# The second layer's modulation: row sums on VectorE and one matmul per condition, in place of eight matmul steps

## The chip, the core and the metric

The kernel runs on one core of a Trainium2 chip. The metric is the device time of one execution in microseconds (us); lower is better. Before the change the median of three runs is 1642.9 us (1642.58 to 1646.06).

## The reference

Two layers of a transformer trunk over 512 latent tokens (x) and 256 context tokens (ctx), width 1024, everything in fp32. Cut to what matters here:

```python
def modulation(cond, w, b):
    return jnp.split(jax.nn.silu(cond) @ w + b, 6, axis=-1)

for l in range(DEPTH):
    last = l == DEPTH - 1
    sh1, sc1, gt1, sh2, sc2, gt2 = modulation(c, w_mod[l], b_mod[l])           # for x
    csh1, csc1, cgt1, csh2, csc2, cgt2 = modulation(c_ctx, w_mod[l], b_mod[l]) # for ctx
    h  = rms_norm(x, g_norm1[l]) * (1 + sc1) + sh1
    hc = rms_norm(ctx, g_norm1[l]) * (1 + csc1) + csh1
    ...                              # projection w_in, three head groups, their norms
    x = x + gt1 * mix_out(...)       # w_o
    if not last: ctx = ctx + cgt1 * mix_out(...)
    x = x + gt2 * sq_relu_mlp(rms_norm(x, g_norm2[l]) * (1 + sc2) + sh2, w_fc1[l], w_fc2[l])
    if not last: ctx = ctx + cgt2 * sq_relu_mlp(...)
```

A modulation is thus silu(cond), a vector of 1024, times a matrix of 1024 by 6144, for two conditions (c and c_ctx) with the same matrix. In the second layer ctx gets only its first norm (csh1, csc1); its other four vectors are not used.

## The kernel before, in words

**Layout.** Activations stand transposed: 128 features on the partitions, 768 tokens (512 of x, then 256 of ctx, `SEGS`) along the row. KC = 8 blocks of 128 features make the width of 1024.

**Large products.** Weights come in chunks of 128 output features (`wraw`, 512 KB each). ScalarE (or VectorE) rounds one half at a time to `whi`, VectorE (or GpSimd, called POOL) subtracts to get `wlo`; four halves of each, so two chunks, have room. Activations are split in the same way into `hh`/`hl`, `oh`/`ol`, `gh`/`gl`. `gemm` and `steps` (L527 to L550) issue, for each of the eight blocks, three matmuls into one PSUM bank (`psmm`): hi by hi, hi by lo, lo by hi. A chunk for both kinds of token is 24 matmuls of 512 columns and 24 of 256. In the MLP, four groups `g` of eight chunks of the first product (`hh`) and eight of the second (`gh`) follow each other. The first is evacuated by `f_evac` (ScalarE `rl` and `gh`, VectorE `sqf` and `gl`), the second by VectorE, which adds into `x`.

**Modulation** (`modulation`, L406). The matrix is cut into three thirds: shift and scale of the first norm; gate of the first sub-layer and shift of the second norm; scale of the second norm and last gate. Each third has two halves of 1024 columns. For each half and each of eight row blocks, two tiles `wm` of 128x512 are loaded, and four small matmuls take the silu vectors `sil` (32 columns, two of them in use) as weights and 256 columns of `wm` each, into four groups of 32 PSUM rows of one bank `psm`; eight row blocks accumulate. These four matmuls are called a group below. Then the bank is copied out (`row`), transposed (`psmt`) and added to the bias (`modc`); for the scales `amod` is made. `mods` (L956) runs, in the first layer, thirds 1 and 2 of that layer after flags set in the projections, and right behind them all three thirds of the second layer.

**What sets the order.** The program is written out ahead by a planner. `_Model` keeps the time at which each engine would be free by a table of costs (`_Engine._cost`, L210) and delays (`WAIT`); `_Order.run` (L289) steps through generators in order of priority, and each yields a condition or a time. Higher priorities are the attention's streams (0 to 2) and the norms; `mods` has 4, `main` with the large products 5. Copies and subtractions go to the engine that the model finds free first (`quickest`, L465). At the end all instructions are issued sorted by the model's start time (`emit`, L170). So a cost in the table can move instructions everywhere after it, and each engine then runs its queue in that order. `SLACK` (3 us) and `LATE` (0.4 us) are margins added to modelled times. Loads are issued on SP's queue; `wm` has two buffers of its own, `wraw` two.

Of the kernel before, what the change touches and what calls it, by code (L numbers as in the profile page):

```python
# [8 lines left out]
F32 = mybir.dt.float32  # L9
F32R = mybir.dt.float32r  # L10
AF = mybir.ActivationFunctionType
ALU = mybir.AluOpType

P = 128
D = 1024
KC = D // P
# [12 lines left out]
V_G1, V_G2, V_GO, V_CW, V_CB, V_NQ, V_NK, V_WQ, V_WK = 0, 8, 16, 24, 30, 32, 33, 34, 35  # L29
# [3 lines left out]
M_SH1, M_SC1, M_GT1, M_SH2, M_SC2, M_GT2 = 0, 8, 16, 24, 32, 40  # L33
# [12 lines left out]
LATE = 400.0  # L46
SLACK = 3000.0


B_HI, B_LO, B_SM, B_SC, B_RM = 100.0, 400.0, 9999.0, 4000.0, 700.0  # L50
# [132 lines left out]
class _Engine:  # L183
# [26 lines left out]
    def _cost(self, op, n, outs, ins, k):  # L210
        if self._name == "PE":
            part, self._md.part = self._md.part, (ins[0].shape[0] > 64, outs[0].shape[0] > 32)
            c = 0.0 if part == self._md.part else 190.0
            if op == "transpose":
                return c + 109.0
            if ins[0].dtype == F32R:
                return c + max(n / 2.4 + 13.6, 110.0)
            return c + (4 * n / 2.4 if outs[0].shape[0] > 32 else 105.0)
        if self._name == "DMA":
            return outs[0].shape[0] * n * 4 / 360.0  # L220
        scalars = sum(1 for x in ins if x.shape[1:] == (1,) or list(x.shape[1:]) == [1]) if n > 1 else 0
        if self._name == "Activation":
            acc = 93.0 if k.get("accum_out") is not None else 0.0
            return (52.0 if ins[0].space == bass.MemoryType.PSUM else 93.0) + 0.8333 * n + 93.0 * scalars + acc
        if self._name == "Pool":
            return 149.0 + 2.104 * n + (128.0 + 0.4 * n if op == "tensor_scalar" else 0.0)
        if op == "reciprocal":
            return 69.0 + 6.25 * n
        return 69.0 + (0.52 if op == "tensor_scalar" else 1.0417) * n + 61.0 * min(scalars, 1)
# [85 lines left out]
def hybrid_trunk(ctx: ExitStack, tc: tile.TileContext, a: dict, out: bass.AP):  # L315
    nc = tc.nc
    md = _Model()
    vec, act, pool, pe, dma = (_Engine(md, e, n) for e, n in (
        (nc.vector, "DVE"), (nc.scalar, "Activation"), (nc.gpsimd, "Pool"), (nc.tensor, "PE"), (nc.sync, "DMA")))
# [5 lines left out]
    wp = _Pool(md, ctx.enter_context(tc.tile_pool(name="wp", bufs=2)), 2)  # L325
# [5 lines left out]
    psp = ctx.enter_context(tc.tile_pool(name="psp", bufs=8, space=PS))  # L331
# [3 lines left out]
    flag, res = (lambda: _Flag(md)), (lambda n: _Res(md, n))  # L335
    r_ps = res(8)
    r_pb, r_pt, r_g, r_l, r_mo, r_tb = res(3), res(2), res(NG), res(NL), res(1), res(2)
# [4 lines left out]
    def const(name, shape, src=None):  # L342
        t = cst.tile(shape, F32, name=name, tag=name)
        if src is not None:
            dma.dma_start(t, src)
        return t

    def tmp(name):
        return tp.tile([P, T], F32, name=name, tag="tmp")

    def taken(name):
        return lp.tile([P, T], F32, name=name, tag="long")

    def long(name):
        r_l.take()
        return taken(name)

    def free(t):
        r_l.give(md.last(t))

    cond, ex, sil = const("cond", [P, KC, 2], a["cond"]), tmp("ex")[:, 0:2 * KC], const("sil", [P, KC, 32])
    vecs = const("vecs", [P, DEPTH, NV], a["vecs"])
# [8 lines left out]
    ident = const("ident", [P, P], a["ident"])  # L371
    bmod = const("bmod", [P, DEPTH, 48], a["bmod"])
# [4 lines left out]
    nc.vector.memset(ones, -0.5)  # L377

    nc.vector.memset(sil, 0.0)
    ex = ex.rearrange("p (k s) -> p k s", k=KC)  # L380
    act.activation(ex, cond, AF.Exp, scale=-1.0)
    vec.tensor_scalar(out=ex, in0=ex, scalar1=1.0, scalar2=None, op0=ALU.add)
# [18 lines left out]
    modc = [const(f"modc{l}", [P, 48, 2]) for l in range(DEPTH)]  # L401
    amod = [const(f"amod{l}", [P, 2, KC, 2]) for l in range(DEPTH)]
    f_mod = {(l, i, j): flag() for l in range(DEPTH) for i in range(3) for j in range(2)}


    def modulation(l, third):  # L406
        first = l == 0 and third == 0
        yield r_mo.need()
        r_mo.take()
        q, ahead = [], [(half, k) for half in range(2) for k in range(KC)]  # L410
        for half in range(2):
            yield r_ps.need()
            r_ps.take()
            ps = psp.tile([P, 512], F32, name="psm", tag="ps")[:, 0:256]
            for k in range(KC):
                while ahead and len(q) < (KC if first else 1):
                    src = a["w_mod"][(l, third) + ahead.pop(0)]
                    if first:
                        yield r_g.need(2)
                        r_g.take(2)  # L420
                    wm = [gp.tile([P, 2, 256], F32, name="wm0", tag="g") if first
                          else wp.tile([P, 2, 256], F32, name="wm", tag="wm") for _ in range(2)]
                    for i in range(2):
                        dma.dma_start(wm[i], src[:, 2 * i:2 * i + 2, :])
                    if first and len(ahead) == KC:
                        f_first.set(0.0)
                    if first and not ahead:
                        f_late.set()
                    q.append(wm)
                wm = q.pop(0)  # L430
                yield md.at(*wm) + (0.0 if first else SLACK)
                for j in range(4):
                    pe.matmul(ps[32 * j:32 * j + 32, :], lhsT=sil[:, k, :], rhs=wm[j // 2][:, j % 2, :], start=k == 0,
                              stop=k == KC - 1)
                if first:
                    r_g.give(k=2)
            yield r_l.need()
            row = long("row")
            vec.tensor_copy(row[:, 0:256], ps)
            r_ps.give(md.last(ps))  # L440
            yield md.at(row[:, 0:256])
            yield r_ps.need()
            r_ps.take()
            pt = psp.tile([P, 512], F32, name="psmt", tag="ps")
            for m in range(2):
                pe.transpose(pt[:, P * m:P * m + P], row[:, P * m:P * m + P], ident)
            free(row)
            pv = pt[:, 0:256].rearrange("p (m i j s) -> p i j m s", m=2, i=2, j=2)
            for i in range(2):
                c = third * 16 + 8 * i + 4 * half  # L450
                vec.tensor_tensor(out=modc[l][:, c:c + 4, :].rearrange("p (j m) s -> p j m s", j=2), in0=pv[:, i, :, :, 0:2],
                                  in1=bmod[:, l, c:c + 4].rearrange("p (j m s) -> p j m s", j=2, s=1).to_broadcast([P, 2, 2, 2]),
                                  op=ALU.add)
            which, col, g = {0: (0, M_SC1, V_G1), 2: (1, M_SC2, V_G2)}.get(third, (None, 0, 0))
            if which is not None:
                col, g, c = col + 4 * half, g + 4 * half, slice(4 * half, 4 * half + 4)
                for s in range(2):
                    vec.scalar_tensor_tensor(out=amod[l][:, which, c, s], in0=modc[l][:, col:col + 4, s], scalar=1.0,
                                             in1=vecs[:, l, g:g + 4], op0=ALU.add, op1=ALU.mult)
            f_mod[l, third, half].set()  # L460
            r_ps.give(md.last(pt))
        r_mo.give()


# [59 lines left out]
    def next_chunk():  # L524
        return unused.pop(0)
# [68 lines left out]

    def room(x):

        yield md.slot("DVE", max(md.t, md.ready(x, "DVE", False)), 69.0 + 61.0 + 1.0417 * x.shape[1], [x]) - B_RM

    def norm_tiles():
        return [[hp.tile([P, T], F32R, name=nm, tag="h") for _ in range(KC)] for nm in ("hh", "hl")]  # L600
# [352 lines left out]
                add_square(acc, xs0[k], s0, s1, k == 0)  # L953
            od.spawn(norm(0, 0, xs0, acc, hh, hl, s, SEGS[s], rd[s], True), s)

    def mods(l, f1, f2):  # L956
        yield f1
        if l == 0:
            yield from modulation(l, 1)
        yield f2  # L960
        if l == 0:
            yield from modulation(l, 2)
        if l + 1 < DEPTH:
            for third in range(3):
                yield from modulation(l + 1, third)

    def main():
        for l in range(DEPTH):
# [15 lines left out]
        for l in range(DEPTH):  # L984
            last = l == DEPTH - 1
            w = S if last else T
# [95 lines left out]
                     "b": lambda i: (segs, conv_evac(2, i), 0)}  # L1082
            seq = [kinds[c](i) for c, i in SEQ]

            f_m = flag(), flag()
            od.spawn(mods(l, *f_m), 4)
            att = attention_streams(l, last, units, o_done)

# [80 lines left out]
            xs, acc = [None] * KC, long("acc")  # L1169
# [61 lines left out]
            for g in range(4):  # L1231
# [26 lines left out]
                    c0 = 2  # L1258
                for c in range(c0, KC):
                    wt = next_chunk()  # L1260
                    for sg in segs:
                        yield from gemm(wt, hh, hl, sg, f_evac(c), sg is segs[-1])

                lastg = g == 3
                if lastg and not last:
# [3 lines left out]
                    acc = long("acc")  # L1269
# [126 lines left out]
```

## Time and profile before

| | |
|---|---|
| median of three runs | 1642.9 us |
| profiled execution | 1646.77 us |
| its span, first to last instruction | 1645.0 us |
| TensorE (PE) busy | 1586.5 us, 96% |
| VectorE (DVE) busy | 1002.1 us, 61% |
| ScalarE (ACT) busy | 705.9 us, 43% |
| POOL busy | 135.3 us, 8% |
| mean granted TensorE clock | 0.989 |

The profiled execution is one run among others, so its own time is given beside its span; differences are made against it. Busy times of matmuls overlap, since a matmul starts before the one ahead has ended; what a matmul costs in a full queue is read from the starts of its neighbours. The first layer's projections and attention run from 31 to 333 us, its w_o stage to 414, its MLP to about 994 us; then the second layer follows, with its own MLP from 1281 us.

### The profile page before, as it was taken

The page shows a single profiled execution, that of the slowest core. Times are in us where ns is not written, and L with a number is a line of the kernel's source. Part 1 is how long each engine was busy: PE and PEld are TensorE (multiplying, and loading weights), DVE is VectorE, ACT ScalarE, POOL GpSimd, SP SyncE. Part 2 cuts the span into 40 slices and gives each one's busy share as a digit, 9 for nine tenths or more (in the row PEclk, how much of TensorE's full clock was granted, in tenths as well). Part 3 has the DMA queues.
Part 4 walks back from the last instruction along what each step waited for, and adds up shares of the span by engine and source line. Part 5 has one row for each costly group of instructions (what it writes and reads, how often), then busy time and mean ns, then how long its engine had stood idle before and what let it go on. Part 6 is the DMA issues. An engine that isn't in the chain of part 4 may idle for free.

```text
span 1645.0 us, 24426 instructions
## 1 busy us (share of the span) xinstructions
PE 1586.5 (96%) x9210; PEld 1311.4 (80%) x9210; DVE 1002.1 (61%) x2030; ACT 705.9 (43%) x1415; POOL 135.3 (8%) x183
## 2 busy tenths in 40 slices
PE   5999999999999999999999998999999899999999
PEld 2787888778788888888888887777879788888887
DVE  4799998966743243334334458899987754545452
ACT  4677776744431122122113346667665422323231
POOL 1002121120000000000000001122212000000000
PEclk9999999999999999999999999999999999999999
DMA  9332322345433333333311243312125232323233
GB/s 330 120 118 91 119 65 79 118 153 196 147 120 115 117 106 126 110 121 104 128 65 65 84 147 115 83 52 78 42 68 174 96 103 90 103 90 103 90 103 102
DMA packets 75718, 182.25 MB, mean 111 GB/s; under 512 B 9424, under 2 KB 15824, under 8 KB 75600
## 3 DMA queue, kind: packets, MB, share of 16 engines
q1 hardware_dynamic: 75600, 180.69, 33.5%
q8 instruction: 72, 1.18, 0.3%
q14 instruction: 46, 0.38, 0.1%
HBM read 170.43 MB, written 5.24 MB: 107 GB/s over the span
## 4 chain that ended last, share of the span: by engine, by line
PE 67%; DVE 14%; ACT 5%; issue 3%; DMA 2%; POOL 0%; SPq 0%; DVEq 0%; ACTq 0%; POOLq 0%
PE psmm L207 61%; DVE pb L207 3%; PE psm L207 2%; DVE ptl L207 2%; ACT pb L207 1%; PE pso L207 1%; DVE o L207 1%; PE pst L207 1%; DVE wlo L207 1%; PE sc L207 1%; DVE hl L207 1%; DVE t L207 1%; DVE sm L207 1%; PE psr L207 1%; DVE tn L207 1%
## 5 line engine op out<-in xcount | busy, mean ns | idle before, releaser
L207 PE MATMUL psmm<-hh,whi 128*128 128x512 f32 (+1 forms) x1264 | 461.8, 365 | 10.9 <-ACT hh L207 4.3
L207 PE MATMUL psmm<-hl,whi 128*128 128x512 f32 (+1 forms) x1264 | 446.3, 353 | 1.5 <-DVE hl L207 0.8
L207 PE MATMUL psmm<-hh,wlo 128*128 128x512 f32 (+1 forms) x1264 | 445.4, 352 | 0.9 <-DVE wlo L207 0.7
L207 ACT ACTIVATE whi<-wraw 128x512 fp32r<-128x512 f32 x323 | 202.9, 630 | 426.2 <-PE psmm L207 403.3
L207 DVE TENSOR_TENSOR wlo<-wraw,whi 128x512 fp32r<-128x512 f32 x357 | 246.9, 694 | 127.5 <-ACT whi L207 124.0
L207 PEld LDWEIGHTS psmm<-hh,whi 128*128 128x128 f32 x1264 | 241.4, 191 | 59.9 <-issue 21.6
L207 PE MATMUL psmm<-gh,whi 128*128 128x512 f32 (+1 forms) x768 | 274.8, 358 | 0.0
L207 PE MATMUL psmm<-gh,wlo 128*128 128x512 f32 (+1 forms) x768 | 272.1, 354 | 0.7 <-DVE wlo L207 0.7
L207 PE MATMUL psmm<-gl,whi 128*128 128x512 f32 (+1 forms) x768 | 272.0, 354 | 0.0
L207 PEld LDWEIGHTS psmm<-hh,wlo 128*128 128x128 f32 x1264 | 240.9, 191 | 35.5 <-DVE wlo L207 3.3
L207 PEld LDWEIGHTS psmm<-hl,whi 128*128 128x128 f32 x1264 | 241.6, 191 | 30.7 <-DVE hl L207 3.5
L207 DVE SCALAR_TENSOR_TENSOR x<-psmm,modc,x 128x512 f32<-128x512 f32 (+1 forms) x96 | 63.5, 661 | 191.6 <-PE psmm L207 191.5
L207 PEld LDWEIGHTS psmm<-gh,whi 128*128 128x128 f32 x768 | 145.2, 189 | 28.2 <-issue 8.9
L207 PEld LDWEIGHTS psmm<-gh,wlo 128*128 128x128 f32 x768 | 145.1, 189 | 21.5 <-DVE wlo L207 1.1
L207 ACT ACTIVATE rl<-psmm 128x512 f32<-128x512 f32 (+1 forms) x98 | 50.9, 519 | 257.2 <-PE psmm L207 257.1
L207 PEld LDWEIGHTS psmm<-gl,whi 128*128 128x128 f32 x768 | 145.3, 189 | 19.5 <-issue 0.2
L207 DVE TENSOR_TENSOR sqf<-rl 128x512 f32<-128x512 f32 (+1 forms) x98 | 58.3, 594 | 151.7 <-ACT rl L207 148.3
L207 ACT ACTIVATE pb<-pb,mn 128x513 f32<-128x513 f32 (+3 forms) x96 | 72.1, 752 | 62.8 <-DVE mn L207 57.0
L207 POOL TENSOR_TENSOR acc<-acc,sq 128x256 f32<-128x256 f32 x34 | 30.5, 897 | 676.1 <-ACT sq L207 600.7
L207 PE MATMUL psmm<-oh,whi 128*128 128x256 f32 (+1 forms) x256 | 82.4, 322 | 0.0
L207 PE MATMUL psmm<-oh,wlo 128*128 128x256 f32 (+1 forms) x256 | 79.9, 312 | 2.2 <-DVE wlo L207 2.2
L207 PE MATMUL psmm<-ol,whi 128*128 128x256 f32 (+1 forms) x256 | 79.8, 312 | 0.0
(142 smaller groups left out, 2097.8 us busy)
## 6 DMA issues: line engine op xcount, KB each, us to landing
wraw<-in_w_fc SPq DMA_DIRECT2D x134, 512.0 KB, 3.5
wm<-in_w_mod SPq DMA_DIRECT2D x192, 256.0 KB, 3.9
wraw<-in_w_in SPq DMA_DIRECT2D x33, 512.0 KB, 3.5
wraw<-in_w_o SPq DMA_DIRECT2D x27, 512.0 KB, 3.5
tb<-in_namask SPq DMA_DIRECT2D x24, 256.0 KB, 2.8
sw<-qg SPq DMA_DIRECT2D x40, 64.0 KB, 2.0
kl<-kl SPq DMA_DIRECT2D x12, 192.0 KB, 2.5
x<-in_xT SPq DMA_DIRECT2D x8, 256.0 KB, 4.5
```

Source lines behind the costliest of these rows:

```text
L207: self._md.log.append((s, len(self._md.log), lambda: f(*a, **k)))
```

## The change

In the second layer a new generator `modulation_sums` takes the place of `modulation`. For each tile `wm` VectorE multiplies by the silu value of its row and adds to an accumulator `macc` of 128x512: one TENSOR_SCALAR for the first row block and seven SCALAR_TENSOR_TENSOR for the others, per accumulator, with two accumulators per half and condition. The sum over the 128 partitions is then done by four matmuls per half and condition, with a column of ones as weights (set in an unused place of `sil`). The first third is made for both conditions, the other two for c alone. What follows (`vectors`) is the old tail of `modulation`, moved into a function. The second layer's modulation starts on a new flag, set at the fifth chunk of the first layer's MLP. The planner's cost of a small matmul is 175 ns instead of 105, and the width in `room` is written as 512 where it was the argument's.

```diff
-            return c + (4 * n / 2.4 if outs[0].shape[0] > 32 else 105.0)
+            return c + (4 * n / 2.4 if outs[0].shape[0] > 32 else 175.0)
...
+    nc.vector.memset(sil[:, 6, 16:17], 1.0)
...
+    def modulation_sums(l, third, conds):
+        yield r_mo.need()
+        r_mo.take()
+        tiles = [(half, i, k) for half in range(2) for i in range(2) for k in range(KC)]
+        loaded, onec = [], sil.rearrange("p k s -> p (k s)")
+        def load():
+            if tiles:
+                half, i, k = tiles.pop(0)
+                wm = wp.tile([P, 2, 256], F32, name="wm", tag="wm")
+                dma.dma_start(wm, a["w_mod"][l, third, half, k][:, 2 * i:2 * i + 2, :])
+                loaded.append(wm)
+        load()
+        for half in range(2):
+            accs = {}
+            for i in range(2):
+                for s in conds:
+                    yield r_l.need()
+                    accs[i, s] = long("macc")[:, 0:512]
+                for k in range(KC):
+                    load()
+                    wm = loaded.pop(0)
+                    yield md.ready(wm, "DVE", False) + SLACK
+                    for s in conds:
+                        yield from room(wm)
+                        w, acc = wm.rearrange("p a c -> p (a c)"), accs[i, s]
+                        if k == 0:
+                            vec.tensor_scalar(out=acc, in0=w, scalar1=sil[:, k, s:s + 1], scalar2=None, op0=ALU.mult)
+                        else:
+                            vec.scalar_tensor_tensor(out=acc, in0=w, scalar=sil[:, k, s:s + 1], in1=acc, op0=ALU.mult,
+                                                     op1=ALU.add)
+            yield md.at(*accs.values()) + LATE
+            yield r_ps.need()
+            r_ps.take()
+            ps = psp.tile([P, 512], F32, name="psm", tag="ps")[:, 0:256]
+            for s in conds:
+                for j in range(4):
+                    pe.matmul(ps[32 * j:32 * j + 32, :], lhsT=onec[:, 208 - s:240 - s],
+                              rhs=accs[j // 2, s][:, 256 * (j % 2):256 * (j % 2) + 256], start=s == conds[0], stop=s == conds[-1])
...
+            yield from vectors(l, third, half, ps)
+        r_mo.give()
...
-        yield md.slot("DVE", max(md.t, md.ready(x, "DVE", False)), 69.0 + 61.0 + 1.0417 * x.shape[1], [x]) - B_RM
+        yield md.slot("DVE", max(md.t, md.ready(x, "DVE", False)), 69.0 + 61.0 + 1.0417 * 512, [x]) - B_RM
...
-    def mods(l, f1, f2):
+    def mods(l, f1, f2, f3):
...
         if l + 1 < DEPTH:
+            yield f3
             for third in range(3):
-                yield from modulation(l + 1, third)
+                yield from modulation_sums(l + 1, third, (0, 1) if third == 0 else (0,))
...
+                    if g == 0 and c == 4:
+                        f_m[2].set()
```

How it moves instructions shows at three places. On TensorE, in the first layer's MLP before, a group of four small matmuls stands between the matmuls of a chunk (here of the first product):

```order
L207 MATMUL psmm<-hh,whi 128x256
L207 MATMUL psmm<-hl,whi 128x256
L207 MATMUL psmm<-hh,wlo 128x256
L207 MATMUL psm<-wm,sil 32x256 x4
L207 MATMUL psmm<-hh,whi 128x256
L207 MATMUL psmm<-hl,whi 128x256
```

There are 48 such groups between the w_o stage and the MLP's end. On TensorE in the same stage now, the chunks hold no group, and at the end of each half one join stands, of eight matmuls in the first third and of four in the others:

```order
L207 MATMUL psmm<-gl,whi 128x512
L207 MATMUL psmm<-gh,wlo 128x512
L207 MATMUL psm<-macc,sil 32x256 x8
L207 MATMUL psmm<-gh,whi 128x512
L207 MATMUL psmm<-gl,whi 128x512
L207 MATMUL psmm<-gh,wlo 128x512
L207 MATMUL psmt<-ident,row 128x128 x2
```

There are six joins, the last some 440 matmul instructions ahead of the second layer's first norm. On VectorE, in the second product of the first MLP group, before:

```order
L207 SCALAR_TENSOR_TENSOR x_1121<-psmm,modc_112,x_1121 128x512
L207 TENSOR_TENSOR wlo<-wraw,whi 128x512
L207 SCALAR_TENSOR_TENSOR x_1121<-psmm,modc_112,x_1121 128x256
L207 TENSOR_TENSOR wlo<-wraw,whi 128x512
L207 SCALAR_TENSOR_TENSOR x_1132<-psmm,modc_112,x_1132 128x512
```

And there now, up to the end of the first half:

```order
L207 SCALAR_TENSOR_TENSOR x_1131<-psmm,modc_113,x_1131 128x512
L207 TENSOR_TENSOR wlo<-wraw,whi 128x512
L207 SCALAR_TENSOR_TENSOR x_1131<-psmm,modc_113,x_1131 128x256
L207 TENSOR_TENSOR wlo<-wraw,whi 128x512
L207 SCALAR_TENSOR_TENSOR macc<-wm,sil,macc 128x512 x4
L207 COPY row<-psm 128x256
L207 SCALAR_TENSOR_TENSOR x_1142<-psmm,modc_113,x_1142 128x512
```

Each chunk has gained four sums here; in the second and third third it is two. The copy of the join's result stands right behind the last sums. On TensorE at the end of the first layer's attention (`pso` is its last product, `psmm<-hh` the projections), before:

```order
L207 MATMUL pso<-pth,vst 128x256
L207 MATMUL pso<-ptl,vst 128x256
L207 MATMUL psm<-wm,sil 32x256 x4
L207 MATMUL psmm<-hh,whi 128x256
L207 MATMUL psmm<-hl,whi 128x256
```

And now:

```order
L207 MATMUL pso<-pth,vst 128x256
L207 MATMUL pso<-ptl,vst 128x256
L207 MATMUL psr<-acc,ones 128x256
L207 MATMUL psmm<-hh,whi 128x512
L207 MATMUL psmm<-hl,whi 128x512
```

Behind the last `pso` and ahead of the w_o stage stood 24 projection matmuls of 512 columns and 33 of 256; now it is 54 and 72. In the second layer TensorE's order differs only in its first rows, and VectorE's in eight spots.

## Rows read from the trace of the kernel before

**Rows 1.** Page, busy us, share of span, instructions:
```profile
PE 1586.5 (96%) x9210; PEld 1311.4 (80%) x9210; DVE 1002.1 (61%) x2030; ACT 705.9 (43%) x1415; POOL 135.3 (8%) x183
```
**Rows 2.** Stretches: length, busy PE, PEld, DVE, ACT, POOL; clock, DMA share, GB/s:
```profile
41.00:333.00 292.00, 284.66 (x1899) 235.76 (x1900) 262.28 (x638) 203.77 (x469) 43.53 (x66) 1.00 0.32 102
414.00:994.00 580.00, 576.79 (x3467) 479.65 (x3459) 244.48 (x435) 153.20 (x275) 7.43 (x8) 1.00 0.33 111
```
**Rows 3.** Tiles `psm` and `wm`, 400 to 830 us: durations ns, first and last start:
```profile
L207 PE MATMUL psm<-wm,sil x384: 379/391/404, 405.1 to 824.6; 128*32 128x256 f32 x192
...
DMA to landing us min/median/max: 2.5/3.9/5.3
```
**Rows 4.** TensorE's timeline around one group: start us, us, instruction:
```profile
539.99 0.40 PE L207 MATMUL psmm<-gl,whi 128*128 128x512 f32 x1
540.22 0.39 PE L207 MATMUL psmm<-gh,wlo 128*128 128x512 f32 x1
540.54 0.64 PE L207 MATMUL psm<-wm,sil 128*32 128x256 f32 x8
541.11 0.50 PE L207 MATMUL psmm<-gh,whi 128*128 128x512 f32 x1
541.45 0.39 PE L207 MATMUL psmm<-gl,whi 128*128 128x512 f32 x1
```
**Rows 5.** Stretches of eight chunks, instructions of `psmm`, then of `psm`:
```profile
567.13:640.43 73.30, 69.30 (x386) 58.36 (x385) 0.48 (x1) 7.48 (x15) 1.00 0.35 115
857.94:924.66 66.72, 66.72 (x386) 59.06 (x385) 0.48 (x1) 7.48 (x15) 1.00 0.19 64
...
567.13:640.43 73.30, 5.11 (x64) 1.26 (x64) 0.42 (x1) 1.00 0.35 115
```
**Rows 6.** TensorE's timeline at the start, four groups in one piece:
```profile
14.27 3.10 PE L207 MATMUL psm<-wm,sil 128*32 128x256 f32 x32
```
**Rows 7.** Groups by form on VectorE, 414 to 994 us; the last of the whole span:
```profile
L207 DVE TENSOR_TENSOR wlo<-wraw,whi 128x512 fp32r<-128x512 f32 x141 | 97.0, 690 | 42.3 <-ACT whi L207 40.8
L207 DVE SCALAR_TENSOR_TENSOR x<-psmm,modc,x 128x512 f32<-128x512 f32 x32 | 24.0, 751 | 129.0 <-PE psmm L207 129.0
L207 DVE TENSOR_TENSOR sqf<-rl 128x512 f32<-128x512 f32 x32 | 22.2, 693 | 135.1 <-ACT rl L207 135.1
...
L207 DVE SCALAR_TENSOR_TENSOR x<-psmm,modc,x 128x256 f32<-128x256 f32 x31 | 15.0, 483 | 6.2 <-PE psmm L207 6.1
L207 DVE CAST whi<-wraw 128x512 fp32r<-128x512 f32 x31 | 13.8, 444 | 1.7 <-PE psmm L207 0.8
L207 DVE TENSOR_TENSOR sqf<-rl 128x256 f32<-128x256 f32 x32 | 13.6, 426 | 3.3
...
L207 DVE SCALAR_TENSOR_TENSOR tn<-x,amod,acc 128x512 f32<-128x512 f32 x8 | 5.9, 746 | 0.0
...
L207 DVE TENSOR_SCALAR pb<-pb,sm 128x512 f32<-128x512 f32 x48 | 24.2, 503 | 1.6
```
**Rows 8.** TensorE's timeline at the start of the MLP, idle time in brackets:
```profile
413.82 0.64 PE L207 MATMUL psm<-wm,sil 128*32 128x256 f32 x8
...
417.78 0.48 PE L207 MATMUL psmm<-hh,whi 128*128 128x512 f32 x1 [2.12 <-DVE whi L207]
```
**Rows 9.** TensorE's waits, 414 to 994 us: us, times, longest:
```profile
PE psmm L207 <- DVE wlo L207: 0.9, 2, 0.7
```
**Rows 10.** TensorE's timeline, last attention product and first w_o matmul:
```profile
320.05 0.28 PE L207 MATMUL pso<-ptl,vst 128*128 128x256 f32 x1
...
333.14 0.40 PE L207 MATMUL psmm<-oh,whi 128*128 128x512 f32 x1
```
**Rows 11.** Stretch 420 to 940 us as in rows 2; VectorE's timeline at 405.80:
```profile
420.00:940.00 520.00, 519.88 (x3149) 431.55 (x3148) 206.18 (x375) 126.78 (x231) 0.00 (x0) 1.00 0.32 106
...
405.80 1.23 DVE L207 SCALAR_TENSOR_TENSOR tn<-x,amod,acc 128x512 f32<-128x512 f32 x1
```

More of the change, by code (lines that the diff above doesn't have):

```diff
@@ L403, in hybrid_trunk, with vectors @@
     f_mod = {(l, i, j): flag() for l in range(DEPTH) for i in range(3) for j in range(2)}
+    def vectors(l, third, half, ps):
+        yield r_l.need()
+        row = long("row")
+        vec.tensor_copy(row[:, 0:256], ps)
+        r_ps.give(md.last(ps))
+        yield md.at(row[:, 0:256])
+        yield r_ps.need()
+        r_ps.take()
+        pt = psp.tile([P, 512], F32, name="psmt", tag="ps")
+        for m in range(2):
+            pe.transpose(pt[:, P * m:P * m + P], row[:, P * m:P * m + P], ident)
+        free(row)
+        pv = pt[:, 0:256].rearrange("p (m i j s) -> p i j m s", m=2, i=2, j=2)
+        for i in range(2):
+            c = third * 16 + 8 * i + 4 * half
+            vec.tensor_tensor(out=modc[l][:, c:c + 4, :].rearrange("p (j m) s -> p j m s", j=2), in0=pv[:, i, :, :, 0:2],
+                              in1=bmod[:, l, c:c + 4].rearrange("p (j m s) -> p j m s", j=2, s=1).to_broadcast([P, 2, 2, 2]),
+                              op=ALU.add)
+        which, col, g = {0: (0, M_SC1, V_G1), 2: (1, M_SC2, V_G2)}.get(third, (None, 0, 0))
+        if which is not None:
+            col, g, c = col + 4 * half, g + 4 * half, slice(4 * half, 4 * half + 4)
+            for s in range(2):
+                vec.scalar_tensor_tensor(out=amod[l][:, which, c, s], in0=modc[l][:, col:col + 4, s], scalar=1.0,
+                                         in1=vecs[:, l, g:g + 4], op0=ALU.add, op1=ALU.mult)
+        f_mod[l, third, half].set()
+        r_ps.give(md.last(pt))
@@ new lines, in modulation_sums @@
+    def modulation_sums(l, third, conds):
[12 more added lines that the diff above has]
+            accs = {}
+            for i in range(2):
+                for s in conds:
+                    yield r_l.need()
+                    accs[i, s] = long("macc")[:, 0:512]
[12 more added lines that the diff above has]
+            yield md.at(*accs.values()) + LATE
+            yield r_ps.need()
+            r_ps.take()
+            ps = psp.tile([P, 512], F32, name="psm", tag="ps")[:, 0:256]
[3 more added lines that the diff above has]
+                              rhs=accs[j // 2, s][:, 256 * (j % 2):256 * (j % 2) + 256], start=s == conds[0], stop=s == conds[-1])
+            for t in accs.values():
+                free(t)
+            yield from vectors(l, third, half, ps)
+        r_mo.give()
@@ L436, in modulation @@
                     r_g.give(k=2)
[L437 to L461, printed above, removed]
+            yield from vectors(l, third, half, ps)
         r_mo.give()
@@ L1083, in main @@
             seq = [kinds[c](i) for c, i in SEQ]
-            f_m = flag(), flag()
+            f_m = flag(), flag(), flag()
             od.spawn(mods(l, *f_m), 4)
```

## The prediction

> **What bounds the kernel now.** I read the page's first part, the busy time by engine, to see which engine fills the span: TensorE is busy 96% of it [rows 1]. An average over stages can mislead, so the second view is the table of stretches. The first layer's MLP runs from 414 to 994 us; TensorE is busy 576.8 of those 580 us at granted clock 1.00, VectorE only 244.5 [rows 2]. The attention before it (41 to 333) looks different: VectorE is busy 262.3 of 292 us, TensorE 284.7. So in the MLP time is a sum over TensorE's queue, and in the attention two engines are close to full.
>
> Third, the instructions of tile `psm` from 400 to 830 us: 384 matmul records [rows 3]. The timeline shows eight records to one group (four instructions, one for each group of 32 PSUM rows) [rows 4], so 384/8 = 48 groups: 3 thirds by 2 halves by 8 row blocks, all of the second layer's modulation. Every one stands in the first layer's w_o stage or MLP.
>
> **What one group costs.** Its busy time is the wrong number, since records overlap. I take it from neighbours' starts. Two matmuls of 512 columns follow each other by 540.22 - 539.99 = 0.23 us. Across a group, the last one before starts at 540.22, the second after at 541.45: 1.23 us, where two steps would be 0.46. The group costs 0.77 us [rows 4]. A check from another view: eight chunks with 64 `psm` records (8 groups) take 73.30 us, eight with none 66.72, with the same 386 matmuls of `psmm` in both [rows 5]. That is 6.58/8 = 0.82 us a group, one pair of transposes included.
>
> **Removed.** 48 x 0.77 = 37.0 us of TensorE's queue.
>
> **Added on TensorE.** 32 matmuls: six joins, two of eight instructions (two conditions in the first third) and four of four. A join of four costs 0.77 as before. For eight, the second four must be bounded: 0.57 us, the start of the group to the next matmul [rows 4], or 3.10/4 = 0.78 where 32 records ran in one piece at the start of the program [rows 6]. I take the middle, 0.67: 4 x 0.77 + 2 x (0.77 + 0.67) = 6.0 us, ends 5.8 and 6.2. The Trainium skill, page "TensorEngine Tiling (Array Packing)", section "Key Properties", says that changing the tiling mode drains the engine; by it the second four, in the same mode, pay no change, and the joins come to 5.8, against 6.2 if every four paid alike. [Rows 4] side with the rule, [rows 6] do not, and it moves the sum by 0.2 us.
>
> Net on TensorE: 37.0 - 6.0 = 31.0 us.
>
> **What of that is not on the path.** One stall of 2.12 us stands at 417.78, where TensorE waits for VectorE's `whi` in the second norm [rows 8]. VectorE is held there by the norm's own chain, so two groups ahead of it (405.1 and 413.8) [rows 3, 8] only filled a wait. In the changed order that place has none: I count 2 x 0.77 = 1.5 us as not won. Ends: 0 (VectorE gets there earlier too) and 2.1.
>
> **Added on VectorE.** 16 sums of eight terms: 16 TENSOR_SCALAR and 112 SCALAR_TENSOR_TENSOR of 128x512. The first kind took 503 ns in this shape, the second 746 ns (`tn<-x,amod,acc`, all operands in SBUF like the new one) [rows 7]: 8.0 + 83.6 = 92 us. VectorE has 580 - 244.5 = 335 us free in the stage, so the question is only whether it is free at the right moments. The order puts four sums into each of 16 chunks and two into each of 32. A chunk of the first product costs VectorE two `wlo` (1.38), one `whi` (0.44), `sqf` of both widths (0.69 + 0.43) and `gl`, the same shapes, put at the same 1.12: 4.1 us. With four sums it is 7.1, and TensorE needs 66.72/8 = 8.34 us for the chunk. A chunk of the second product has two `wlo` and two `x` (0.75 + 0.48): 2.6, with four sums 5.6. So this work lies beside TensorE, with 1.2 us to spare in the tightest chunk. A delay of one burst of sums (3 us) also meets cover: weights are split two chunks ahead (about 8 us), and `gl` of the last chunk is wanted only after seven of eight row blocks of the next product, some 21 x 0.23 = 4.8 us. If that cover went, TensorE would wait by the excess.
>
> **The new wait.** At each join TensorE waits for VectorE's last sum, and behind it stand all later matmuls. The planner leaves a margin of 0.4 us (`LATE`). Ends: nothing, as VectorE's other hand-overs in the stage (0.9 us of waiting for `wlo` in 580 us) [rows 9], and one late sum at each, 6 x 0.75 = 4.5. I take 1.0, near the row. `COPY row<-psm` then holds VectorE's queue until the join is through, about 1.5 us; that is inside the spare time above.
>
> The same six halves keep their transposes and small additions, so these cancel. DMA bytes are the same. The tile loads now wait for VectorE instead of TensorE on SP's queue; each landed in 3.9 us, 5.3 at most [rows 3], issued one tile ahead, which fits into a chunk with two tiles.
>
> **The clock.** 414 to 994 runs at 1.00 [rows 2], and the eight chunks without these groups run at 1.00 too [rows 5]. No term.
>
> **What the re-planning does.** The planner's cost for small matmuls goes from 105 to 175 ns, so the first layer's attention is laid out anew, although its work is the same. In the order the last `pso` now has 54 projection matmuls of 512 columns and 72 of 256 behind it, against 24 and 33 before: 54 x 0.23 + 72 x 0.12 = 21.1 us of TensorE work instead of 9.5 (the step of 256 is what a chunk leaves: (8.34 - 24 x 0.23)/24 = 0.12). Before, 13.1 us lie between the two events [rows 10]. If the attention now ends as much sooner, nothing changes; TensorE idles 7.3 us in all of that stage [rows 2], which is the most there is to win. If VectorE sets the attention's length, TensorE runs dry for up to 21.1 - 9.5 = 11.6 us. I take 0, because TensorE's own work fills 97% of the stage, with ends -7.3 and +11.6. In the second layer TensorE's order is unchanged nearly throughout and VectorE's differs in eight spots: 0.
>
> **Sum.** 31.0 - 1.5 - 1.0 = 28.5 us. The profiled execution took 1646.8 us (span 1645.0, 1.8 outside): 1646.8 - 28.5 = 1618.3. It lies 3.9 above the median of the runs, 1642.9; on that scale 1614.4 us. That is what I forecast.
>
> **Rivals.**
> 1. The attention pays. VectorE decides its length and the moved projections find TensorE idle: 1614.4 + 11.6 = 1626. For it: VectorE is busy 90% of the stage. Against: TensorE is busy 97% there, so most of the moved work has no idle time to leave. Chance 14%.
> 2. The new layout is better: the 7.3 us of idle time halve or go, 1614.4 - 7.3 = 1607. Less work of the projections and of the group norms falls together near 330 us. Chance 9%.
> 3. VectorE's queue becomes the bound in the MLP, the slower side. A sum at its head waits for its tile, and `wlo`, `sqf` and `x` behind wait with it. Each chunk has two tiles. With a wait w per tile, the tightest chunks need 7.1 + 2w against 8.34, eight of them; the others of four sums 5.6 + 2w, eight; the 16 first-product chunks of two sums 5.6 + 2w. At w = 1.65 us this loses 16 + 4 + 9 = 29 us and eats the gain; at w = 2 it is about 22 + 10 + 20 = 52, so 1614.4 + 52 = 1666. Against: 3.9 us of landing within a chunk of 8.34. The sums can also stretch: one SCALAR_TENSOR_TENSOR took 1.23 us at 405.80 near work of POOL. POOL has 0.00 us from 420 to 940 [rows 11], so nothing stretches them there. The Trainium skill, "SBUF — State Buffer", says that a VectorE operation with two SBUF inputs and a GpSimd operation lock each other out of a shared port for a whole instruction, a rule against moving work to VectorE; by it too, an idle POOL costs nothing. Chance 4%.
> 4. The change does not bring what it says, because the MLP is paced by its weights and not by TensorE: about 1643. Against it stand the 66.72 and 73.30 us [rows 5]. Chance 2%.
>
> The forecast has 71%, with its own range 1609 to 1621: the ends above for TensorE, the stall and the joins make it 1612 to 1619, and 2.5 us either way are for a layout that is nearly neutral. The range that should hold the time 8 times in 10 adds most of rivals 1 and 2: 1606 to 1625. A measurement of this kernel tells about 0.2%, 3.3 us, from no change. Faster: forecast and rivals 1 and 2, 94%. Same: rival 4 and the middle of rival 3, 3%. Slower: the rest of rival 3, 3%.
>
> **What the profile of the changed kernel would show.** Eight chunks of the MLP with sums beside them take about 67.5 us, not 73.3. `macc` operations take about 0.75 us and VectorE is some 335 us busy in the MLP. TensorE waits for `macc` under 0.75 us at each of six joins. The second layer's stages keep their lengths. From 41 to 333 us, the order's new layout ends the projections within 7 us of where they ended. I would be wrong if TensorE shows waits for `wlo`, `gl` or `x` in the MLP, if a group turns out to have hidden something else behind it, or if the attention moved by more than its 7 us of idle time.

## The result, and the profile after

The changed kernel takes 1630.62 us (median of four runs, 1629.09 to 1631.59); the kernel before, timed beside it, took 1644.48 (1642.58 to 1646.62). The ratio is 0.9915, with an interval of 0.9897 to 0.9932. The gain is 13.9 us, where 28.5 were forecast, and the time lies above the range.

The page's first part, busy us by engine, against [rows 1]:

```profile
PE 1561.1 (96%) x8890; PEld 1313.7 (81%) x8890; DVE 1089.0 (67%) x2159; ACT 704.3 (43%) x1414; POOL 137.3 (8%) x184
```

TensorE has 320 matmul records less (a small matmul leaves two), VectorE 129 instructions more and 86.9 us more work. The stretches, columns as in [rows 2]: the attention, the MLP, eight MLP chunks with sums and a join of eight, eight with sums and a join of four, and 60 us in the attention's middle:

```profile
41.00:344.00 303.00, 287.99 (x1893) 238.15 (x1893) 268.85 (x643) 205.20 (x474) 47.71 (x70) 0.99 0.30 97
421.00:976.00 555.00, 549.43 (x3155) 479.63 (x3154) 326.08 (x561) 153.00 (x275) 9.79 (x9) 0.99 0.36 118
...
499.74:567.91 68.17, 68.17 (x404) 59.58 (x403) 42.48 (x71) 10.30 (x17) 1.29 (x1) 1.00 0.38 124
...
704.28:772.02 67.74, 67.74 (x397) 59.33 (x395) 40.80 (x72) 21.14 (x39) 0.00 (x0) 1.00 0.37 121
...
100.00:160.00 60.00, 53.48 (x365) 43.63 (x365) 54.34 (x145) 43.54 (x104) 10.21 (x20) 0.96 0.33 106
```

The third and fourth lines are the change at work: 68.17 and 67.74 us, where eight chunks took 73.30 with the groups and 66.72 with none [rows 5]. The last line is the trouble. The same 60 us before:

```profile
100.00:160.00 60.00, 59.31 (x398) 48.40 (x397) 54.50 (x141) 45.04 (x107) 10.20 (x18) 1.00 0.32 100
```

VectorE is as busy as it was (54.3 and 54.5), but TensorE runs 5.8 us less, at a granted clock of 0.96. The attention's end, against [rows 10]: the last attention product and the first w_o matmul on TensorE's timeline.

```profile
318.57 0.28 PE L207 MATMUL pso<-ptl,vst 128*128 128x256 f32 x1
...
344.36 0.40 PE L207 MATMUL psmm<-oh,whi 128*128 128x512 f32 x1
```

The attention itself ends 1.5 us sooner (318.57 against 320.05), but the moved projections then take 25.8 us where 13.1 stood. By the starts of the stages' first matmuls in the two profiled executions (spans 1645.0 and 1629.8), the difference of 15.2 us is: start -0.7, projections and attention +12.0, w_o -4.6, MLP -24.0, second layer +2.2. The w_o stage and the MLP together give 28.6, as much as the whole kernel was to gain, and the attention took 12.0 of it back.

Where it waits: TensorE's longest waits from 41 to 344 us (what waited, for what, us in all, times, longest; `sc` are scores, `pst` and `pstc` transposes of the probabilities).

```profile
PE pstc L207 <- DVE t L207: 2.5, 1, 2.5
PE sc L207 <- DVE o L207: 1.4, 1, 1.4
PE pst L207 <- DVE pb L207: 1.3, 3, 0.5
PE sc L207 <- DVE ptl L207: 1.2, 1, 1.2
PE psmm L207 <- ACT hh L207: 1.2, 1, 1.2
```

Before, in its stretch 41 to 333, the list was headed by:

```profile
PE psr L207 <- ACT sqq L207: 1.5, 2, 1.1
PE psmm L207 <- DVE ptl L207: 1.1, 1, 1.1
PE psr L207 <- DVE ptl L207: 0.8, 1, 0.8
PE pst L207 <- DVE t L207: 0.5, 2, 0.3
```

Summed over the stage from 41 us on, TensorE's waits of over 0.15 us make 14.5 us, against 6.6; 11.0 and 4.6 of them end with VectorE. The longest wait can be read step by step. First TensorE's timeline, then VectorE's up to the same moment:

```profile
151.11 0.65 PE L207 MATMUL psr<-sqq,heads 128*128 128x256 f32 x2
...
153.27 0.28 PE L207 MATMUL scx<-kl,qst 128*128 128x256 f32 x1
156.03 0.47 PE L207 MATMUL pstc<-ident,pbc 128*128 128x128 f32 x1 [2.48 <-DVE t L207]
```

```profile
151.54 0.69 DVE L207 TENSOR_TENSOR wlo<-wraw,whi 128x512 fp32r<-128x512 f32 x1
152.51 0.16 DVE L207 TENSOR_TENSOR sm<-sm 128x1 f32<-128x1 f32 x1 [0.28 <-ACT sm L207]
...
153.63 0.35 DVE L207 TENSOR_SCALAR pbc<-pbc,sm 128x256 f32<-128x256 f32 x1
153.90 0.68 DVE L207 TENSOR_TENSOR sw<-sw,sinT 128x512 f32<-128x512 f32 x1
154.69 0.69 DVE L207 TENSOR_TENSOR qg<-t,sw 128x512 f32<-128x512 f32 x1
155.29 0.68 DVE L207 SCALAR_TENSOR_TENSOR t<-psr,t 128x512 f32<-128x512 f32 x1
156.01 0.69 DVE L207 SCALAR_TENSOR_TENSOR sqq<-t,sqq 128x512 f32<-128x512 f32 x1
```

The transposes `pstc` wait until VectorE has read a `psr` out of PSUM (`t<-psr,t`). VectorE comes to that at 155.29, behind a weight split, a softmax's sums and two operations of a rotation, with hardly a gap between them. VectorE had as much to do as before; it did it in an order that made TensorE wait. Before, the same 20 `pstc` between 118 and 198 us waited for nothing. At the end of this wait the granted clock fell to its lower level, 1.2 GHz, for 6.8 us:

```profile
155.40:162.20 6.80, 5.88 (x15) 4.53 (x16) 5.86 (x12) 3.42 (x7) 0.18 (x1) 0.50 0.19 70
```

Matmuls of 512 columns follow each other by 0.43 us there (158.02 and 158.45) and by 0.23 from 162.51 on. At half speed the 6.8 us lose 3.4 us at most, since the wait itself reaches into them.

In the MLP the new parts are the accumulators (tile `macc`, durations min/median/max ns, first and last start), and TensorE's waits from 421 to 976:

```profile
L207 DVE SCALAR_TENSOR_TENSOR macc<-wm,sil,macc x112: 739/747/1532, 476.9 to 875.2; 128x512 f32<-128x512 f32 x112
...
L207 PE MATMUL psm<-macc,sil x64: 378/379/404, 538.0 to 876.9; 128*32 128x256 f32 x64
L207 DVE TENSOR_SCALAR macc<-wm,sil x16: 479/481/483, 474.7 to 841.8; 128x512 f32<-128x512 f32 x16
```

```profile
PE psmm L207 <- ACT hh L207: 3.1, 2, 2.7
PE psmm L207 <- ACT whi L207: 1.3, 1, 1.3
PE psmm L207 <- DVE wlo L207: 0.6, 2, 0.4
PE psmt L207 <- DVE row L207: 0.3, 1, 0.3
```

No wait for `macc` is among them. The 2.7 for `hh` belongs to the layout: it falls into the second norm, and VectorE's timeline ahead of it shows two pairs of the MLP's own operations put before the norm's last `tn`:

```profile
436.84 0.69 DVE L207 TENSOR_TENSOR sqf<-rl 128x512 f32<-128x512 f32 x1
437.64 0.69 DVE L207 TENSOR_TENSOR gl<-sqf,gh 128x512 fp32r<-128x512 f32 x1
438.25 0.69 DVE L207 TENSOR_TENSOR sqf<-rl 128x512 f32<-128x512 f32 x1
439.04 0.69 DVE L207 TENSOR_TENSOR gl<-sqf,gh 128x512 fp32r<-128x512 f32 x1
439.65 0.48 DVE L207 SCALAR_TENSOR_TENSOR tn<-x,amod,acc 128x256 f32<-128x256 f32 x1
```

### The profile page after: what moved, and what is told of

Same layout as the page of the kernel before. It is cut to its first block, busy times and chain, and to the rows that moved or that the text cites. A ratio compares the mean times of both kernels' runs of the same rounds, so it can differ in the third digit from the quotient of the medians.

```text
span 1629.8 us, 23969 instructions
## 1 busy us (share of the span) xinstructions
PE 1561.1 (96%) x8890; PEld 1313.7 (81%) x8890; DVE 1089.0 (67%) x2159; ACT 704.3 (43%) x1414; POOL 137.3 (8%) x184
## 4 chain that ended last, share of the span: by engine, by line
PE 70%; DVE 15%; ACT 7%; DMA 5%; issue 3%; SPq 0%; POOL 0%; DVEq 0%; ACTq 0%; POOLq 0%
PE psmm L207 64%; DVE pb L207 3%; PE pso L207 2%; DVE ptl L207 2%; ACT pb L207 1%; DVE wlo L207 1%; DMA wm<-in_w_mod 1%; PE pst L207 1%; ACT hh L207 1%; PE sc L207 1%; DVE hl L207 1%; PE psr L207 1%; DVE tn L207 1%; DVE o L207 1%; DMA wraw<-in_w_o 1%
## 5 line engine op out<-in xcount | busy, mean ns | idle before, releaser
L207 PEld LDWEIGHTS psmm<-gh,wlo 128*128 128x128 f32 x768 | 145.2, 189 | 20.9 <-DVE wlo L207 0.8
L207 DVE SCALAR_TENSOR_TENSOR macc<-wm,sil,macc 128x512 f32<-128x512 f32 x112 | 81.3, 754 | 1.0 <-DMA wm<-in_w_mod 0.2
```

The lines of the kernel that those rows point to most:

```text
L207: self._md.log.append((s, len(self._md.log), lambda: f(*a, **k)))
```

## The experiments

The theory: the sums are worth what was forecast, and the loss comes from the planner's new cost of 175 alone, because it lays out the attention anew. The first rival to it: the sums cost TensorE something in the MLP that the forecast missed. A second question is what in the new layout costs the time: the projection work left behind the last `pso` (rival 1 of the prediction), or VectorE's order ahead of it. Each kernel was timed beside the kernel before, which took 1644.0 us next to the first four kernels below and 1645.51 next to the last four.

**The sums in the old layout** (the change, with the old cost and the old slot in `room` for everything that existed before; TensorE's order is that of before up to the MLP).

```diff
-            return c + (4 * n / 2.4 if outs[0].shape[0] > 32 else 175.0)
+            return c + (4 * n / 2.4 if outs[0].shape[0] > 32 else 105.0)
...
-        yield md.slot("DVE", max(md.t, md.ready(x, "DVE", False)), 69.0 + 61.0 + 1.0417 * 512, [x]) - B_RM
+        yield md.slot("DVE", max(md.t, md.ready(x, "DVE", False)), 69.0 + 61.0 + 1.0417 * (512 if len(x.shape) > 2 else x.shape[1]), [x]) - B_RM
```

> The change with the planner's two numbers left as before (105 ns for a small matmul, the width in `room` as it was for the callers that were there): only the row sums on VectorE and their joins are new, and the first layer's attention is laid out as before. If the re-planned attention took the missing part of the gain: first w_o matmul at 333 us as before, MLP about 24 us shorter than before, 26 to 29 us faster in all. If the sums themselves bring only half of what was forecast (fillers of waits, contention on VectorE): 13 to 16 us faster, like the changed kernel.

Measured: 1615.11 us (1613.37 to 1616.78), ratio 0.9826 [0.9811, 0.984]: 28.9 us faster than before and 15.5 faster than the change as made. It is the best complete version here. Its stretches, columns as in [rows 2]:

```profile
100.00:160.00 60.00, 59.40 (x398) 48.44 (x398) 54.53 (x141) 45.03 (x107) 10.18 (x17) 1.00 0.32 101
...
691.25:759.00 67.75, 67.75 (x396) 59.31 (x395) 40.80 (x72) 21.15 (x39) 0.00 (x0) 1.00 0.36 121
```

The middle of the attention is that of before, and up to the w_o stage every engine's order in the trace is that of before (VectorE has one memset more); the eight chunks are those of the changed kernel. So the loss isn't in the sums.

**The cost alone**, in the kernel before:

```diff
-            return c + (4 * n / 2.4 if outs[0].shape[0] > 32 else 105.0)
+            return c + (4 * n / 2.4 if outs[0].shape[0] > 32 else 175.0)
```

> The kernel before with only the planner's cost of a small matmul at 175 ns: no sums. If the re-planned attention is the loss: first w_o matmul near 344 us, MLP as before (about 579 us), 8 to 11 us slower in all. If the re-planning is neutral and the sums are at fault: no difference.

Measured: 1658.95 us (1656.69 to 1660.49), ratio 1.0091 [1.0076, 1.0106]: 15.0 us slower, with no instruction added or removed. The middle of its attention, and the two events of [rows 10]:

```profile
100.00:160.00 60.00, 53.00 (x369) 43.31 (x368) 54.53 (x147) 43.70 (x104) 10.23 (x20) 0.98 0.33 107
```

```profile
318.04 0.28 PE L207 MATMUL pso<-ptl,vst 128*128 128x256 f32 x1
...
343.82 0.40 PE L207 MATMUL psmm<-oh,whi 128*128 128x512 f32 x1
```

The two halves of the change add up: 28.9 - 15.0 = 13.9, which is what the whole gained; each has an interval of some 2.5 us either way. The width in `room` was not tried by itself. TensorE's order up to the w_o stage is here that of the changed kernel but for two `psr`, and VectorE's differs in some operations of the norms, so little is left for the width to do.

The loss is larger than the 8 to 11 us expected. The profiled execution was the fastest of the four and shows 9.9 us of it: start of the projections +1.2, attention +9.5, w_o -4.6, MLP +5.8, second layer -1.9. The MLP was expected to stay as it was; its 5.8 us lie mostly in its first eight chunks (below).

**The groups not issued.** The kernel before, planned as it was, but of each half's eight groups of the second layer's modulation the first seven (42 in all) are planned and not issued; the modulation's vectors of the second layer are therefore not the reference's.

```diff
-                    pe.matmul(ps[32 * j:32 * j + 32, :], lhsT=sil[:, k, :], rhs=wm[j // 2][:, j % 2, :], start=k == 0,
-                              stop=k == KC - 1)
+                    o, w = ps[32 * j:32 * j + 32, :], {"lhsT": sil[:, k, :], "rhs": wm[j // 2][:, j % 2, :]}
+                    if l > 0 and k < KC - 1:
+                        md.op("PE", *pe._parse("matmul", (o,), w))
+                    else:
+                        pe.matmul(o, start=k == 0 or l > 0, stop=k == KC - 1, **w)
```

> The kernel before, its order kept, but of the second layer's modulation only the last of eight row blocks is issued on TensorE, in each of the six halves (the planner still counts all; the modulation is then wrong by the seven missing blocks). 42 groups of 0.77 us leave TensorE's queue, 32.3 us, and VectorE gains no work. If a group costs 0.77 us wherever it stands: 31 to 32 us faster. If the groups ahead of and within the second norm's waits only fill those waits: about 6 of them bring nothing, 26 to 28 us faster. The difference of this kernel and the first one, beyond the joins, is what the sums on VectorE cost.

Measured: 1614.69 us (1614.14 to 1616.88), ratio 0.9826 [0.9811, 0.984]: 29.3 us for 42 groups, 0.70 each overall, between the two cases expected. By the price of 0.77 they are 32.3, so some 3 us of them filled waits, where 1.5 were assumed; the interval is some 2.4 us either way. The stretch of its MLP that answers to the one above, columns as in [rows 2]:

```profile
690.46:758.21 67.75, 67.75 (x396) 59.31 (x395) 30.94 (x59) 21.16 (x39) 0.00 (x0) 1.00 0.38 125
```

It holds one group instead of a join of four, and no sums: the same 67.75 us with 9.9 us less on VectorE. Over the whole kernel it is 0.4 us faster than the sums in the old layout, inside the intervals. The sums cost TensorE nothing that these runs can tell.

**Another cost, 120**, in the sums' old layout, to see whether 175 is special (the edit is against that kernel, as are the next two):

```diff
-            return c + (4 * n / 2.4 if outs[0].shape[0] > 32 else 105.0)
+            return c + (4 * n / 2.4 if outs[0].shape[0] > 32 else 120.0)
```

> As the first kernel, with the cost at 120 ns. In this order 69 matmuls of 512 and 72 of 256 columns of the projections stand behind the last `pso`, 24.3 us of TensorE work, where the order before has 9.4 and the changed one 20.9. If what is left behind the attention decides, because VectorE sets the attention's length: first w_o matmul at 333 + 15 = 348 us, 11 to 15 us slower than the first kernel. If the loss at 175 was one unlucky place and not the left-over work: within 4 us of the first kernel.

Measured: 1634.94 us (1633.1 to 1636.48), ratio 0.995 [0.9933, 0.9966]: 19.8 us slower than with 105. The work left behind the last `pso` is 24.3 us against 9.4, which would explain 15. Its 60 us from 160 on show what else there is: TensorE busy 51.95, and the clock at 0.89.

```profile
160.00:220.00 60.00, 51.95 (x340) 42.36 (x341) 51.99 (x131) 34.94 (x87) 7.99 (x12) 0.89 0.33 106
```

**Cost 100**, and **another pace** (`B_SC` of 4000 halved: the margin by which scores are issued ahead of a free VectorE or ScalarE; cost 105), both in the same kernel:

```diff
-            return c + (4 * n / 2.4 if outs[0].shape[0] > 32 else 105.0)
+            return c + (4 * n / 2.4 if outs[0].shape[0] > 32 else 100.0)
```

> The row sums with the cost at 100 ns: 36 matmuls of 512 and 48 of 256 columns stand behind the last `pso`, 13.9 us, against 9.4 at 105. If the work left behind decides: first w_o matmul at 333.4 + 4.5 = 338 us, 3 to 5 us slower than the sums in the old layout. If the layout's loss is chance: 333 or any other value up to 344.

```diff
-B_HI, B_LO, B_SM, B_SC, B_RM = 100.0, 400.0, 9999.0, 4000.0, 700.0
+B_HI, B_LO, B_SM, B_SC, B_RM = 100.0, 400.0, 9999.0, 2000.0, 700.0
```

> The row sums at cost 105 with the attention paced differently: the margin `B_SC`, by which scores are issued ahead of a free VectorE, at 2 us instead of 4. 24 matmuls of 512 and 24 of 256 stand behind the last `pso`, 8.3 us instead of 9.4. If the work left behind decides: the first w_o matmul within 2 us of 332, the time the same as that of the sums in the old layout or up to 2 us less. If the margin was what kept VectorE fed: last `pso` later and the kernel 3 us or more slower.

Measured: 1621.47 us (1619.63 to 1623.32), ratio 0.9852 [0.9831, 0.9873], and 1639.88 us (1638.93 to 1640.9), ratio 0.9964 [0.995, 0.9977]. Cost 100 leaves 13.9 us over, 4.5 more than 105, and its attention takes 9.0 more. The halved pace leaves the least of all, 8.3, and its attention takes 14.1 more. So the left-over work does not set the stage's length.

**Less work on VectorE**, in the new layout (cost 175) and in the old one. The first 18 chunks are planned as before, but their `wlo` is not made, and the third matmul reads `whi` in its place; the projections of the first layer thus lack the weights' low part. POOL's share of these subtractions goes too.

```diff
-                minus(lo, src, hi.bitcast(F32))
+                c.no_lo = c in chunks[:18]
+                if c.no_lo:
...
+                    md.op(eng._name, *eng._parse("tensor_tensor", (), k))
+                else:
+                    minus(lo, src, hi.bitcast(F32))
...
+            if w.no_lo:
...
+                               nc.tensor.matmul(ps, lhsT=h, rhs=x, start=False, stop=e)))
+            else:
+                pe.matmul(ps, lhsT=lo[:, kc], rhs=ah[k][:, s0:s1], start=False, stop=k == end)
```

> The changed kernel (cost 175, `room` as before) with the same taken away: 23 subtractions of 0.69 us, 15.9 us, less on VectorE. If VectorE sets the attention's length and TensorE runs dry beside it: last `pso` from 318.6 to about 304, idle time of TensorE in the stage from 15 to under 5 us, first w_o matmul from 344 to 331 to 334, some 10 us or more gained, twice or three times what the old layout gains. If the new order's own waits are the loss: under 4 us gained.

> The row sums in the old layout, order kept, but the first layer's 18 projection chunks make no `wlo` (the third matmul of each block reads `whi` instead, so these products are off by their low part). 24 subtractions of 0.69 us leave VectorE, 16.6 us, and 12 leave POOL; TensorE has as many matmuls as before. If VectorE sets the attention's length: last `pso` near 304 to 310 us instead of 320, but the first w_o matmul only at 328 to 330 instead of 333.4, since TensorE has just 5.4 us of idle time to give there. If the attention's length comes from the order and its chains of waits: both move by less than 3 us.

Measured: 1621.33 us (1620.85 to 1621.82), ratio 0.9851 [0.9833, 0.9869], and 1609.9 us (1608.66 to 1611.15), ratio 0.9782 [0.9762, 0.9801]. The attention stage gains 10.5 us in the new layout (314.1 to 303.6) and 5.0 in the old (302.3 to 297.3). That is the twofold gain expected if VectorE sets the length, but TensorE's waits in the new layout fall only to 9.1 us, not under 5, and the last `pso` of the old layout only to 314.8, not to 304 to 310. Busy time from 41 us to the stage's end, columns as in [rows 2], the new layout first:

```profile
41.00:334.00 293.00, 283.41 (x1892) 237.07 (x1885) 254.37 (x623) 205.43 (x475) 29.70 (x57) 0.99 0.31 99
```

```profile
41.00:328.00 287.00, 282.81 (x1909) 236.12 (x1909) 251.50 (x621) 203.63 (x470) 26.62 (x54) 1.00 0.32 103
```

TensorE has as many matmuls as with the subtractions, and fewer waits: they end mostly with VectorE. But taking 14.5 us off VectorE (268.85 to 254.37) leaves the longest waits of the new layout where they were:

```profile
PE pstc L207 <- DVE t L207: 2.5, 1, 2.5
PE sc L207 <- DVE o L207: 1.4, 1, 1.4
PE sc L207 <- DVE ptl L207: 1.2, 1, 1.2
```

These three thus did not come from the amount of work on VectorE; that they come from the order of the two queues is what is left, not a test of its own.

All runs by stage, from the starts of each stage's first matmul (idle: TensorE's waits of over 0.15 us, from 41 us on; left over: projection work behind the last `pso` in the order, at steps of 0.228 and 0.119 us, which the prediction rounds to 0.23 and 0.12; first half: the first eight chunks of the MLP):

| kernel | last pso | attention | its idle | left over | w_o | MLP | its first half |
|---|---|---|---|---|---|---|---|
| before | 320.1 | 302.1 | 6.6 | 9.4 | 81.3 | 578.9 | 79.4 |
| changed | 318.6 | 314.1 | 14.5 | 20.9 | 76.7 | 554.9 | 78.7 |
| sums, old layout | 320.3 | 302.3 | 5.4 | 9.4 | 79.9 | 549.8 | 73.9 |
| cost 175 alone | 318.0 | 311.6 | 14.4 | 20.9 | 76.7 | 584.7 | 84.2 |
| sums, cost 120 | 324.5 | 324.5 | 23.0 | 24.3 | 77.2 | 550.7 | 74.8 |
| sums, cost 100 | 323.0 | 311.3 | 13.4 | 13.9 | 76.6 | 549.4 | 73.7 |
| sums, pace 2000 | 334.1 | 316.4 | 14.0 | 8.3 | 76.1 | 555.5 | 79.3 |
| groups not issued | 319.9 | 302.2 | 6.4 | 9.4 | 79.4 | 549.2 | 74.8 |
| 175, less VectorE | 308.7 | 303.6 | 9.1 | 20.9 | 76.6 | 554.6 | 78.0 |
| old, less VectorE | 314.8 | 297.3 | 3.8 | 9.4 | 80.3 | 549.7 | 74.0 |

The attention column goes with the idle column, and the rest of the difference with the clock. Over the stage it was 0.96 with cost 120, 0.98 at the halved pace (the one kernel clearly out of line in the two columns), 0.99 in the three kernels with 175, and 1.00 in the others. For the changed kernel 7.9 us more of idle time and at most 3.4 us for the clock make 11.3 of the 12.0 us measured.

## Why the prediction was wrong

**The group's price held.** 0.77 us from the neighbours' starts; in eight chunks seven groups less gave 73.30 - 67.75 = 5.55, or 0.79 each.

**The joins: fours right, eights a little high.** Eight chunks with a join of four and the transposes take 67.75 - 66.72 = 1.03 us more than with none, with a join of eight in the changed kernel 68.17 - 66.72 = 1.45 (its second stretch with one, 567.91 to 636.53, took 68.6 and holds the wait of 0.3 for `row`). The forecast had 0.77 and 1.44 for the joins without the transposes; the second four cost about 0.4, under the 0.57 taken as its lower end.

**Net of 28.5 us: right, in part by luck.** The sums in the old layout gave 28.9. What only filled waits was put at 1.5 (about 3 by the groups not issued), and the waits at the joins at 1.0 (none for `macc`, 0.3 for `row`); the two errors nearly cancel.

**The work on VectorE was hidden, as forecast.** 747 and 481 ns where 746 and 503 were taken, 326 us busy where 335 were forecast, no wait for `macc`; rival 3 did not come about. One sentence of it fails: POOL was not idle all through the MLP. It made one `wlo` at 543.69 (1.29 us), and the sum that started beside it at 543.99 took 1.53 us. TensorE did not wait for it.

**The step that failed** is "What the re-planning does": "I take 0, because TensorE's own work fills 97% of the stage, with ends -7.3 and +11.6". The cost alone takes 15.0 us. The reason was wrong in kind. The 7.3 us of idle time say how much a better order could win; they say nothing of how much a worse one can lose. VectorE is busy 90% of the stage [rows 2], and in the new order TensorE's waits that end with VectorE grew from 4.6 to 11.0 us, though VectorE has the same work (54.3 and 54.5 us in the 60 above). The end of +11.6 was very near the attention's +12.0, so rival 1, at 14%, was the case that came, and what it said against itself (no idle time to leave) was the same error. Yet its reason holds only in part, and its near hit is partly luck: the left-over work did run behind the last `pso`, but costs 100 and 120 lost more than it says, and the halved pace lost 14 us without it. What holds in all runs is the idle time that the order causes, most of it in waits for VectorE, with the lower clock on top in some.

**What no case had** is a smaller effect of the layout at the start of the MLP. The changed kernel takes 78.7 us for the first eight chunks, the sums in the old layout 73.9. The cost alone shows the same 4.8 us (84.2 against 79.4) and the same wait for `hh` (2.35 us), so this too is the layout. In the changed kernel that wait is 2.70 us. The first 75 us of the MLP, the changed kernel first:

```profile
421.03:496.03 75.00, 70.13 (x361) 59.86 (x360) 50.82 (x92) 29.95 (x57) 2.35 (x2) 0.93 0.27 88
```

```profile
413.33:488.33 75.00, 72.59 (x391) 62.40 (x392) 53.34 (x96) 32.54 (x63) 1.19 (x1) 0.95 0.29 94
```

TensorE is idle 2.5 us longer, and the clock is lower. The w_o stage, cut off sooner, gives 3.2 of the 4.8 back. Against the old layout the attention thus costs 11.8 us, the w_o stage and the MLP 1.9, and the second layer about 2; less 0.8 at the start, that is the 15 us between the two profiled executions.

Open: why each order puts its waits where it does. The runs give no rule by which a cost could be chosen ahead. 105 was the best of the four tried, and all four other layouts (costs 100, 120 and 175, the halved pace) lengthen the attention; why the order before is so good isn't on record. The first eight chunks of the second layer's MLP, the same work everywhere, take 54.9 to 58.1 us; that goes with the clock: 54.9 to 55.7 in the five kernels where it is 0.94 in them, 55.8 and 57.4 where it is 0.91, 57.7 to 58.1 where it is 0.88. Why it falls longer in some isn't shown.

## What to carry to other kernels

A constant in a planner's cost table is an edit of its own: try it apart from the work that it comes with, for it lays out everything anew, also the stages in which the work doesn't change. A busy share of 97% on the bounding engine limits what a new order can win, not what it can lose; where a second engine is busy 90%, price a new order at several per cent of the stage on the losing side: the four new layouts here lost 3 to 7%. Work that moves from a full engine to a half-empty one at known hand-overs, as the sums here, can be summed up row by row: here it came to 28.9 us against 28.5, with single terms off by 1 to 1.5 us.

## What was not expected of the hardware

A wait of about 2.5 us stands at a fall of the granted clock in two of these kernels and not in a third. In the changed kernel it was 1.2 GHz from 155.4 to 162.2 us, at the end of a wait of 2.48 us. With the cost alone the same wait ended at 156.50, and the clock was at 1.2 GHz from 158.2 to 161.6. With cost 100 a wait of 2.66 us ended at 228.16, and the whole attention ran at 2.4 GHz:

```profile
41.00:341.90 300.90, 286.82 (x1904) 235.00 (x1901) 270.15 (x644) 203.40 (x472) 46.67 (x67) 1.00 0.31 99
```

What a fall costs comes on top of the idle time: at most 3.4 us in the changed kernel's attention.

In a join of eight, the second four small matmuls cost about 0.4 us (68.17 against 67.74 us for eight chunks), where four by themselves cost 0.77 among the chunk's matmuls [rows 4].
